# SwiGLU with stationary tokens: another order of products and output blocks, VectorE and ScalarE in written order, and a quarter of the turning transfers issued from POOL

## The chip, the core and the metric

One core of one Trainium2 chip runs the kernel. The metric is the device time in microseconds; three runs of the kernel before took 1253.64, 1248.87 and 1252.88 us, median 1252.88. TensorE (PE in the profile) multiplies, VectorE (DVE), ScalarE (ACT) and GpSimd (POOL) do the elementwise work, and SyncE (SP) issues most transfers (DMAs).

## The reference, cut to what matters

A trunk of two layers over 512 tokens of width 1024 in float32: a recurrent layer (RG-LRU), then a dilated attention layer; each ends in a SwiGLU, and the change is in that SwiGLU alone, which runs twice.

```python
D_MODEL = 1024; SEQ = 512; FFN_HIDDEN = 2816
def swiglu(h, w_in, w_out):
    g, u = jnp.split(h @ w_in, 2, axis=-1)
    return (jax.nn.silu(g) * u) @ w_out
...
h = h + swiglu(rms_norm(h, a_ffn_norm[i]), a_ffn_w_in[i], a_ffn_w_out[i])
...
h = h + swiglu(rms_norm(h, b_ffn_norm[j]), b_ffn_w_in[j], b_ffn_w_out[j])
```

## The kernel before

Every float32 operand is held as two parts, hi (rounded to the type that PE multiplies fast) and lo (the rest), and a product of two operands is three matmuls (`mm3`, L183): hi by hi, and the two mixed ones. Making the parts is called a split: ScalarE casts hi (named wh, xh, gh or T), VectorE subtracts for lo (wl, xl, gl).

`swiglu` (L581) computes 2816 hidden columns. The first 256 are done plainly (four blocks of 24 matmuls, `plain_block`); `plain_pair` applies the gate to them. The norm's factors per token come from `norm_factors` behind the first block and are spread by `norm_rows` behind the third: VectorE makes dgh and dgl (L330, L331), and PE multiplies them with ones (L335, L336) in its written order. The other 2560 columns are done in five groups of 512, counted by q from 0 to 4 and called quarters here. Each replaces the eight products of a 2 x 2 block scheme (halves of the tokens, halves of the input width, gate and up weights) by seven, with sums of weights and of inputs in their place: S1, GA, S2, GB, S3, S4 and UB. In these the tokens are stationary on PE and 512 weight columns stream, so a result has tokens in its 128 partitions. Seven products of 24 matmuls each make a quarter.

The sums of inputs are T1 to T4 (`make_t1` and so on, with d0, d1, x22 and t between); B11, B21 and B22 are parts of the input itself. The weights are fetched into GA, GB, S1, S3 and UB (`fetch`, L637); S1 and S3 take a second transfer from POOL that adds (L646), and further sums (S1 += GA for S2, GB += S1 for S4) are made on VectorE (L656), in quarter 0 by `split_weights` just ahead of the splits of S2 and S4. A product adds onto PSUM banks that an earlier one left: S2, S3 and UB onto GA's, S4 onto S1's. What stood there is copied off before (`S.copy`, L749), and behind S3 an addition reads S1's banks (L751). `gate` (L703) applies silu behind GB and S4, and `results` (L710) multiplies by the up part and turns 32 x 32 blocks on VectorE (L716).

To be the input of the product with `w_out`, the quarter's result must have its hidden columns in the partitions. `land` (L718) finishes the turn by 16 transfers of 64 KB from SBUF to SBUF (L726) into gl (in the last quarter into T2), and then splits the chunk into gh and gl (T1 and T2), four times ScalarE and four times VectorE (L729, L730). An output block O (`out_block`, L761) multiplies a piece of `w_out` by the chunk of the quarter before, and VectorE subtracts the result from the residual h (L772, in quarter 0 L774). The last chunk is multiplied by eight blocks at the very end ("last").

What sets the order: the strings in ORDERS (L40 to L42) give the order of products and O in each quarter; PE follows the written order in the whole loop (`manual_schedule`, L780). VectorE and ScalarE are put in order by a scheduler, which lets instructions marked `high_priority` (the splits of weights, the norm) go ahead. SP's and POOL's queues run in order too. `Stream` loads weight pieces four ahead and splits them two ahead; three pieces of wh and wl are in flight, so the split of a piece waits until PE has done the piece three before.

Of the kernel before, what the change touches and what calls it, by code (L numbers as in the profile page):

```python
# [15 lines left out]
F32 = mybir.dt.float32  # L16
# [3 lines left out]
AF = mybir.ActivationFunctionType  # L20
ALU = mybir.AluOpType
# [3 lines left out]
T = 512  # L25
# [147 lines left out]
def trunk(tc, A, out):  # L173
# [29 lines left out]
    class Ffn:  # L203


        def __init__(self, wi, wo, gain):
            self.gain = gain
            self.wi, self.wo = A[wi], A[wo]
            self.split = None
            self.steps = []  # L210
            for j in range(2):
                self.steps += [("plain", j, b, add_pieces([self.wi[b]])) for b in (j, HB + j)]
            for q, names in enumerate(ORDERS):
                waiting = list(range(0, 8, 2 if q else 4))
                for name in names.split():
                    if name == "O":
                        m = waiting.pop(0)
                        if q:
                            w = self.wo[m:m + 2, :, 512 * q - 256:512 * q + 256]
                        else:  # L220
                            w = self.wo[m:m + 4, :, :256]
                        self.steps.append(("out", q, m, add_pieces([w.rearrange("b q c -> q b c")])))
                    else:
# [17 lines left out]
    with tc.tile_pool(name="keep", bufs=1) as kp, tc.tile_pool(name="wts", bufs=3) as wp, \  # L241
# [339 lines left out]
        def swiglu(fp, p, after):  # L581
# [9 lines left out]
            for i, x in enumerate(sums):  # L591
                homes[f"T{i + 1}"] = [x[:, 2 * w:2 * w + 2].rearrange("q a (b t) -> q (a b) t", b=2) for w in range(2)]
            chunks = {}
            d0, d1, x22, t = (x[:, 2 * i:2 * i + 2].rearrange("q a (b t) -> q (a b) t", b=2).bitcast(F32)
                              for x in chunk() for i in range(2))
            late = slice(256, 512)

            def differences(k, dst):
# [9 lines left out]
                for i in range(4):  # L608
                    V.scalar_tensor_tensor(dst[:, i], src(i), gain(p.gain, i), x[:, i], ALU.mult, op)

            def negated(n, src):
                hi, lo = homes[n]
                S.activation(hi, src, AF.Copy, scale=-1.0)
                V.scalar_tensor_tensor(lo, src, -1.0, hi.bitcast(F32), ALU.mult, ALU.subtract)
# [33 lines left out]
            def split_weights(q, name, kk, hi, lo):  # L648
                n = name[:2]
                home = {"S2": "S1", "S4": "GB"}.get(n, n)  # L650

                def half(n):
                    return raws[q, n][:, :, 256 * kk:256 * kk + 256]

                def add(n, other):
                    V.tensor_tensor(half(n), half(n), half(other), ALU.add)  # L656

                with tc.high_priority():
                    if q == 0 and n in ("S2", "S4"):
                        add(*{"S2": ("S1", "GA"), "S4": ("GB", "S1")}[n])  # L660
                    r = half(home).rearrange("q b (k c) -> q k b c", k=2)
                    hi, lo = (x.rearrange("q (k b c) -> q k b c", k=2, b=4) for x in (hi, lo))
                    S.copy(hi, r)  # L663
                    V.tensor_tensor(lo, r, hi.bitcast(F32), ALU.subtract)  # L664
                    if q and n in ("GA", "GB"):
                        add(*{"GA": ("S1", "GA"), "GB": ("GB", "S1")}[n])
# [5 lines left out]
            p.split = split_weights  # L672
            rows, plain, acc = [], {}, {}

            def pair_tile(name="e"):
                return temps.tile([128, 2, T], F32, name=name)

            def plain_block(j, b, i):
                ps = bank("mm" if plain else "X")
                wh, wl = ws.get(i)  # L680
                for k in range(KB):
                    c = slice(128 * k, 128 * k + 128)
                    mm3(ps, (wh[:, c], wl[:, c]), (xh[k], xl[k]), k == 0, k == KB - 1)
                plain[b] = ps
                with tc.high_priority():
                    if b == 0:
                        p.r = norm_factors(fp)
                    elif b == 1:
                        rows.append(norm_rows(temps, p.r, keep=fp))

            def plain_pair(j):
                if j == 0:
# [16 lines left out]

            def results(q, half, up, part):  # L710
                if q not in turned:
                    turned[q] = fp.tile([128, 16, 4, 32], F32, name="wt", bufs=1)
                for i in range(2):
                    j = 2 * half + i
                    V.scalar_tensor_tensor(part[:, i], up[i], p.r[:, j:j + 1], part[:, i], ALU.mult, ALU.mult)  # L715
                    p.mark = V.transpose(turned[q][:, :, j], part[:, i].rearrange("q (b i) -> q b i", i=32))  # L716

            def land(q):  # L718
# [4 lines left out]
                src = turned.pop(q).rearrange("q (m b) t i -> q m b (t i)", b=4)  # L723
                for a in range(4):
                    for b in range(4):
                        nc.sync.dma_start(lo[32 * b:32 * b + 32, :, 128 * a:128 * a + 128].bitcast(F32),  # L726
                                          src[32 * a:32 * a + 32, :, b])
                for m in range(4):
                    S.copy(hi[:, m], lo[:, m].bitcast(F32))  # L729
                    V.tensor_tensor(lo[:, m], lo[:, m].bitcast(F32), hi[:, m].bitcast(F32), ALU.subtract)  # L730
# [44 lines left out]

            for n in ("GA", "GB", "S1", "S3", "UB"):
                fetch(0, n)
            early = {0: make_t1, 1: lambda: (make_t2(), make_t3()), 2: make_t4, 3: lambda: plain_pair(0),
                     4: lambda: (halve(d0, *homes["T4"]), plain_pair(1))}
            with tc.manual_schedule(engines={mybir.EngineType.PE}):  # L780
                for s, (kind, *what) in enumerate(p.steps):
                    {"plain": plain_block, "product": product, "out": out_block}[kind](*what)
                    early.get(s, lambda: None)()
# [565 lines left out]
```

## Time and profile before

| | |
|---|---|
| runs | 1253.64, 1248.87, 1252.88 us |
| the profiled execution | 1252.88 us, its span 1251.0 us, 1.9 us around it |
| PE | 5403 matmuls in the profile, busy 94% |
| VectorE, ScalarE, POOL | busy 68%, 50%, 13% |
| granted clock of PE, mean | 0.975 |
| first SwiGLU | from about 152 to 541 us of the span |
| second SwiGLU | from about 869 us to the end |

A row of a timeline gives the start in us, the duration, the engine, the line, the operation with its tiles (out<-in) and shapes, and in brackets the idle time ahead of it and what ended it. A row of the waits gives who waited for whom, the total in us, how often, and the longest. A matmul of 512 columns shows as 0.39 us but overlaps the next; what counts is the distance between starts. In the groups, "x60 | 63.2, 1054" is 60 instructions, 63.2 us busy, 1054 ns each.

### The profile page before, as it was taken

The numbers are of one execution on the slowest core, as the hardware profiler recorded it, in microseconds if no ns is written. First come the engines' busy times: TensorE is split into PE (matmuls) and PEld (weight loads), VectorE is DVE, ScalarE is ACT, GpSimd is POOL, SyncE is SP. The second block draws the span as 40 slices with busy tenths as digits, with TensorE's granted clock in tenths as the row PEclk, the third lists the DMA queues.
The fourth block names the chain that finished last, engine by engine and source line by source line (L and its number), as shares of the span: only waits on it lengthen the run. The fifth ranks groups of instructions, "written<-read, shape, count | busy, mean of one in ns | idle before, by whom it ended". The sixth has DMA issues, their size and how long they took to land.

```text
span 1251.0 us, 15052 instructions
## 1 busy us (share of the span) xinstructions
PE 1180.6 (94%) x5403; PEld 966.0 (77%) x5403; DVE 853.3 (68%) x1525; ACT 626.9 (50%) x901; POOL 166.6 (13%) x181
## 2 busy tenths in 40 slices
PE   9999998999898989799999999999998999989897
PEld 6787886777786868688888888898776877778676
DVE  8987696757575757878564676757957575757563
ACT  6795463434334343465555677646534343433431
POOL 4210011010100000010411333440110101010000
PEclk9999999999898989899999999999999999989898
DMA  7543395574655512332988667435975737464123
GB/s 245 127 121 101 101 284 155 162 181 131 167 149 153 165 51 69 101 123 89 211 183 178 136 134 169 91 77 129 260 192 147 201 110 187 130 168 134 49 65 117
DMA packets 96715, 179.61 MB, mean 144 GB/s; under 512 B 8705, under 2 KB 32129, under 8 KB 96641
## 3 DMA queue, kind: packets, MB, share of 16 engines
q1 hardware_dynamic: 77904, 132.86, 33.0%
q0 software_dynamic: 17584, 44.57, 20.6%
q10 hardware_dynamic: 1152, 1.23, 0.3%
q8 instruction: 43, 0.70, 0.2%
q14 instruction: 32, 0.25, 0.1%
HBM read 164.99 MB, written 2.10 MB: 134 GB/s over the span
## 4 chain that ended last, share of the span: by engine, by line
PE 76%; DVE 9%; ACT 6%; issue 3%; DMA 3%; SPq 2%; POOL 1%; DVEq 0%; ACTq 0%; POOLq 0%
PE ps L186 20%; PE ps L187 20%; PE ps L185 20%; PE ps L1012 5%; PE ps L1013 5%; PE ps L1014 5%; SPq L726 2%; DVE wl L664 2%; ACT wh L663 1%; ACT wh L133 1%; DVE S L656 1%; DVE xc L466 1%; PE ps L1091 1%; DVE e L715 1%; PE ps L1178 1%
## 5 line engine op out<-in xcount | busy, mean ns | idle before, releaser
L133 ACT CAST wh<-wr 128x1024 fp32r<-128x1024 f32 (+2 forms) x136 | 131.9, 970 | 182.4 <-PE ps L186 116.9
L185 PE MATMUL ps<-gh,wh 128*128 128x512 f32 x288 | 120.7, 419 | 23.7 <-ACT gh L729 18.1
L186 PE MATMUL ps<-gl,wh 128*128 128x512 f32 x288 | 121.5, 422 | 11.9 <-DVE gl L730 11.0
L663 ACT CAST wh<-S 128x1024 fp32r<-128x1024 f32 x60 | 63.2, 1054 | 126.5 <-PE ps L187 84.2
L185 PE MATMUL ps<-wh,xh 128*128 128x512 f32 x320 | 124.7, 390 | 1.9 <-DVE e L715 1.9
L187 PE MATMUL ps<-wh,xl 128*128 128x512 f32 x320 | 124.5, 389 | 0.0
L186 PE MATMUL ps<-wl,xh 128*128 128x512 f32 x320 | 124.5, 389 | 0.0
L140 DVE TENSOR_TENSOR wl<-wr,wh 128x1024 fp32r<-128x1024 f32 (+2 forms) x93 | 100.7, 1084 | 30.0 <-ACT wh L133 29.8
L646 POOL DMA_DIRECT2D S<-in_f_in x40 | 48.2, 1286 | 541.7 <-DMA S<-in_f_in 372.1
L187 PE MATMUL ps<-gh,wl 128*128 128x512 f32 x288 | 119.9, 416 | 0.0
L664 DVE TENSOR_TENSOR wl<-S,wh 128x1024 fp32r<-128x1024 f32 x60 | 73.5, 1224 | 49.4 <-ACT wh L663 49.4
L185 PE MATMUL ps<-wh,T 128*128 128x512 f32 x240 | 95.8, 399 | 6.5 <-ACT e L749 6.5
L185 PE MATMUL ps<-xh,wh 128*128 128x512 f32 x256 | 101.0, 396 | 0.5 <-ACT xh L294 0.5
L187 PE MATMUL ps<-xh,wl 128*128 128x512 f32 x256 | 100.0, 391 | 0.8 <-DMA wl<-in_w_in 0.8
L186 PE MATMUL ps<-xl,wh 128*128 128x512 f32 x256 | 100.1, 391 | 0.1
L772 DVE TENSOR_TENSOR h<-h,ps 128x512 f32<-128x512 f32 x64 | 43.7, 682 | 80.2 <-PE ps L187 80.1
L186 PE MATMUL ps<-wl,T 128*128 128x512 f32 x240 | 93.6, 390 | 0.0
L187 PE MATMUL ps<-wh,T 128*128 128x512 f32 x240 | 93.4, 389 | 0.0
L1012 PE MATMUL ps<-wh,xh 128*128 128x512 f32 x224 | 91.5, 408 | 0.0
L185 PEld LDWEIGHTS ps<-gh,wh 128*128 128x128 f32 x288 | 58.6, 204 | 41.5 <-ACT gh L729 21.5
L1014 PE MATMUL ps<-wh,xl 128*128 128x512 f32 x224 | 87.7, 392 | 0.0
L1013 PE MATMUL ps<-wl,xh 128*128 128x512 f32 x224 | 87.3, 390 | 0.0
(280 smaller groups left out, 2676.7 us busy)
## 6 DMA issues: line engine op xcount, KB each, us to landing
S<-in_f_in SPq DMA_DIRECT2D x40, 512.0 KB, 4.5
S<-in_f_in POOLq DMA_DIRECT2D x40, 512.0 KB, 7.9
wr<-in_f_out SPq DMA_DIRECT2D x36, 512.0 KB, 4.3
wr<-in_w_q SPq DMA_DIRECT2D x28, 512.0 KB, 6.8
wl<-in_w_q POOLq DMA_DIRECT2D x28, 512.0 KB, 7.6
GA<-in_f_in SPq DMA_DIRECT2D x20, 512.0 KB, 3.9
GB<-in_f_in SPq DMA_DIRECT2D x20, 512.0 KB, 6.0
UB<-in_f_in SPq DMA_DIRECT2D x20, 512.0 KB, 4.5
```

What stands on the lines that cost most here:

```text
L133: nc.scalar.copy(hi[:, c], r[:, c])
L140: a = eng.tensor_tensor(lo[:, c], r[:, c], hi[:, c].bitcast(F32), ALU.subtract)
L185: PE.matmul(ps, wh, xh, start=first, stop=False, skip_group_check=on)
L186: PE.matmul(ps, wh, xl, start=False, stop=False, skip_group_check=on)
L187: PE.matmul(ps, wl, xh, start=False, stop=last, skip_group_check=on)
L646: nc.gpsimd.dma_start(c, p.part(1, q, n == "S1", i), accum_op=ALU.add)
L663: S.copy(hi, r)
L664: V.tensor_tensor(lo, r, hi.bitcast(F32), ALU.subtract)
L772: V.tensor_tensor(by_time(x), by_time(x), in_turn(ps), ALU.subtract)
L1012: PE.matmul(ps[t], xh[k][:, r], wh[:, c], start=k == 0, stop=False)
L1013: PE.matmul(ps[t], xh[k][:, r], wl[:, c], start=False, stop=False)
L1014: PE.matmul(ps[t], xl[k][:, r], wh[:, c], start=False, stop=k == 7)
```

## The change

Three things change, all in `swiglu`. The order strings: GB now stands right behind GA in the middle quarters, two O follow S2, and a new step "L" is the place where the chunk is split (`parts_of`, taken out of `land`); the last quarter ends in three O with an L ahead of the third. The loop runs under a written order for VectorE and ScalarE as well as for PE, without the marks of priority; and T2 and T3 are made together, T4 later, with d0, d1, x22 and t in other tiles. And of the 16 turning transfers, the four with a == 0 are issued from POOL.

```diff
-MIDDLE = "S1.T1 GA.B11 S2.T2 O GB.B21 O S3.T3 O S4.B22 O UB.T4"
-ORDERS = ["GA.B11 GB.B21 O S1.T1 S2.T2 S3.T3 O S4.B22 UB.T4", MIDDLE, MIDDLE, MIDDLE,
-          "S1.T1 GA.B11 S2.T2 O GB.B21 S3.T3 O S4.B22 UB.T4 O O"]
+MIDDLE = "S1.T1 GA.B11 GB.B21 L S2.T2 O O S3.T3 O S4.B22 O UB.T4"
+ORDERS = ["GA.B11 GB.B21 O S1.T1 S2.T2 O S3.T3 S4.B22 UB.T4", MIDDLE, MIDDLE, MIDDLE,
+          "S1.T1 GA.B11 GB.B21 L S2.T2 O S3.T3 S4.B22 UB.T4 O O L O"]
...
-            d0, d1, x22, t = (x[:, 2 * i:2 * i + 2].rearrange("q a (b t) -> q (a b) t", b=2).bitcast(F32)
-                              for x in chunk() for i in range(2))
+            d = turn_tile().rearrange("q a b i -> q (a b i)").rearrange("q (w k t) -> q w k t", w=2, k=4)
+            d0, d1 = (d[:, i] for i in range(2))
+            x22, t = (quarters(pair_tile(n)) for n in ("x22", "t"))
...
-            def make_t2():
+            def make_t23():
                 gained(x22, lambda i: h[4 + i][:, late], 1)
                 combine(t, lambda i: d0[:, i], x22, ALU.add)
-                negated("T2", t)
-
-            def make_t3():
+                S.activation(homes["T2"][0], t, AF.Copy, scale=-1.0)
                 combine(x22, lambda i: h[i][:, late], x22, ALU.subtract)
-                negated("T3", x22)
+                S.activation(homes["T3"][0], x22, AF.Copy, scale=-1.0)
+
+            def low_t23():
+                for n, src in (("T2", t), ("T3", x22)):
+                    hi, lo = homes[n]
+                    V.scalar_tensor_tensor(lo, src, -1.0, hi.bitcast(F32), ALU.mult, ALU.subtract)
...
-                with tc.high_priority():
-                    if q == 0 and n in ("S2", "S4"):
-                        add(*{"S2": ("S1", "GA"), "S4": ("GB", "S1")}[n])
...
+                if q == 0 and n in ("S2", "S4"):
+                    add(*{"S2": ("S1", "GA"), "S4": ("GB", "S1")}[n])
...
-                        nc.sync.dma_start(lo[32 * b:32 * b + 32, :, 128 * a:128 * a + 128].bitcast(F32),
-                                          src[32 * a:32 * a + 32, :, b])
+                        (nc.gpsimd if a == 0 else nc.sync).dma_start(
+                            lo[32 * b:32 * b + 32, :, 128 * a:128 * a + 128].bitcast(F32), src[32 * a:32 * a + 32, :, b])
+
+            def parts_of():
+                hi, lo = chunks[max(chunks)]
                 for m in range(4):
                     S.copy(hi[:, m], lo[:, m].bitcast(F32))
                     V.tensor_tensor(lo[:, m], lo[:, m].bitcast(F32), hi[:, m].bitcast(F32), ALU.subtract)
...
-            early = {0: make_t1, 1: lambda: (make_t2(), make_t3()), 2: make_t4, 3: lambda: plain_pair(0),
-                     4: lambda: (halve(d0, *homes["T4"]), plain_pair(1))}
+            early = {0: make_t1, 1: make_t23, 2: low_t23, 3: lambda: plain_pair(0), 4: lambda: plain_pair(1),
+                     6: lambda: (make_t4(), halve(d0, *homes["T4"]))}
+            ordered = {mybir.EngineType.PE, mybir.EngineType.DVE, mybir.EngineType.Activation}
+            with tc.manual_schedule(engines=ordered):
```

The three places below name lines of their own kernel: L664, L330, L331, L601, L774 and L656 of before are L674, L332, L333, L614, L785 and L667 after the change, L729 is L740, L749 is L760 and L706 is L712.

VectorE at the start of the first SwiGLU, before: the small dependent steps of the norm (nry), then dgh and dgl, with sums for T2 and T3 (gl, here used as room for t and x22) between them and the split of GA's first piece (wl28) among them.

```order
L290 SCALAR_TENSOR_TENSOR nry_1443<-nra_1444,nry_1443 128x4
L609 SCALAR_TENSOR_TENSOR gl_1377<-h2_66,par_74,gl_1377 128x256
L330 TENSOR_SCALAR dgh_1539<-ident_75,nry_1443 128x128 x2
L331 SCALAR_TENSOR_TENSOR dgl_1540<-ident_75,nry_1443,dgh_1539 128x128 x2
L330 TENSOR_SCALAR dgh_1539<-ident_75,nry_1443 128x128
L664 TENSOR_TENSOR wl28_1512<-GA_1378,wh28_1511 128x1024
L331 SCALAR_TENSOR_TENSOR dgl_1540<-ident_75,nry_1443,dgh_1539 128x128
L330 TENSOR_SCALAR dgh_1539<-ident_75,nry_1443 128x128
L614 SCALAR_TENSOR_TENSOR T2_1374<-gl_1377,T2_1374 128x1024
L331 SCALAR_TENSOR_TENSOR dgl_1540<-ident_75,nry_1443,dgh_1539 128x128
```

The same place after the change, from T1's low parts on: the sums t and x22 for T2 and T3, then wl28, and only then the first dgh and dgl.

```order
L297 SCALAR_TENSOR_TENSOR T1_1373<-wt_1376,par_74,T1_1373 128x256 x4
L140 TENSOR_TENSOR wl27_1468<-wr27_1403,wh27_1467 128x1024
L622 SCALAR_TENSOR_TENSOR t_1378<-wt_1376,par_74,x22_1377 128x256 x4
L622 SCALAR_TENSOR_TENSOR x22_1377<-h0_64,par_74,x22_1377 128x256
L622 SCALAR_TENSOR_TENSOR x22_1377<-h1_65,par_74,x22_1377 128x256
L622 SCALAR_TENSOR_TENSOR x22_1377<-h2_66,par_74,x22_1377 128x256
L622 SCALAR_TENSOR_TENSOR x22_1377<-h3_67,par_74,x22_1377 128x256
L674 TENSOR_TENSOR wl28_1511<-GA_1379,wh28_1510 128x1024
L332 TENSOR_SCALAR dgh_1538<-ident_75,nry_1444 128x128
L333 SCALAR_TENSOR_TENSOR dgl_1539<-ident_75,nry_1444,dgh_1538 128x128
```

dgh and dgl, which PE's next matmuls read, moved behind the eight sums and behind wl28.

ScalarE in quarter 2 of the first SwiGLU, before: the copies behind GA (e_2512), S2 (e_2550), the cast of the chunk (gh, L729), and the splits of O (wr68, wr71) and GB.

```order
L663 CAST wh66_2480<-S1_2115 128x1024
L663 CAST wh67_2496<-S1_2115 128x1024
L749 COPY e_2512<-ps_2476 128x512
L133 CAST wh68_2515<-wr68_2478 128x1024
L749 COPY e_2512<-ps_2477 128x512
L663 CAST wh69_2533<-GB_2268 128x1024
L749 COPY e_2550<-ps_2476 128x512
L663 CAST wh70_2553<-GB_2268 128x1024
L749 COPY e_2550<-ps_2477 128x512
L729 CAST gh_2411<-gl_2412 128x512 x4
L133 CAST wh71_2593<-wr71_2531 128x1024
L663 CAST wh72_2611<-S3_2192 128x1024
```

The same quarter after the change, from the copies behind GA (e_2510) on; e_2510 at L712 is GB's gate, wr70 and wr71 are the two O.

```order
L760 COPY e_2510<-ps_2469 128x512
L760 COPY e_2510<-ps_2470 128x512
L673 CAST wh68_2517<-S1_2050 128x1024
L673 CAST wh69_2535<-S1_2050 128x1024
L712 ACTIVATE e_2510<-e_2510,nry_1444 128x512 x2
L740 CAST gh_2412<-gl_2413 128x512 x4
L133 CAST wh70_2563<-wr70_2515 128x1024
L133 CAST wh71_2579<-wr71_2533 128x1024
L760 COPY e_2595<-ps_2469 128x512
L760 COPY e_2595<-ps_2470 128x512
L673 CAST wh72_2600<-S3_2193 128x1024
L673 CAST wh73_2632<-S3_2193 128x1024
```

The cast of the chunk now stands behind GB's gate, and the casts of both O behind it.

VectorE in quarter 0 around the first O, before: wl34 is S1's second piece, wl35 S2's first; L656 are the additions for S2 and S4, and L774 drains O's four blocks.

```order
L705 TENSOR_TENSOR e_1637<-ps_1650,e_1637 128x512
L656 TENSOR_TENSOR S1_1384<-S1_1384,GA_1378 128x4x256
L664 TENSOR_TENSOR wl34_1689<-S1_1384,wh34_1688 128x1024
L656 TENSOR_TENSOR GB_1381<-GB_1381,S1_1384 128x4x256
L656 TENSOR_TENSOR S1_1384<-S1_1384,GA_1378 128x4x256
L705 TENSOR_TENSOR e_1637<-ps_1651,e_1637 128x512
L656 TENSOR_TENSOR GB_1381<-GB_1381,S1_1384 128x4x256
L774 TENSOR_TENSOR h0_64<-h0_64,ps_1692 128x512
L774 TENSOR_TENSOR h1_65<-h1_65,ps_1700 128x512
L774 TENSOR_TENSOR h2_66<-h2_66,ps_1708 128x512
L774 TENSOR_TENSOR h3_67<-h3_67,ps_1716 128x512
L664 TENSOR_TENSOR wl35_1727<-S1_1384,wh35_1726 128x1024
```

The same place after the change.

```order
L785 TENSOR_TENSOR h0_64<-h0_64,ps_1679 128x512
L785 TENSOR_TENSOR h1_65<-h1_65,ps_1687 128x512
L785 TENSOR_TENSOR h2_66<-h2_66,ps_1695 128x512
L785 TENSOR_TENSOR h3_67<-h3_67,ps_1703 128x512
L614 TENSOR_TENSOR wt_1376<-h4_68 128x256
L614 TENSOR_TENSOR wt_1376<-h5_69 128x256
L614 TENSOR_TENSOR wt_1376<-h6_70 128x256
L614 TENSOR_TENSOR wt_1376<-h7_71 128x256
L622 SCALAR_TENSOR_TENSOR wt_1376<-wt_1376,par_74 128x256 x4
L302 TENSOR_TENSOR xl_73<-wt_1376,xh_72 128x4x256
L667 TENSOR_TENSOR S1_1385<-S1_1385,GA_1379 128x4x256
L674 TENSOR_TENSOR wl35_1730<-S1_1385,wh35_1729 128x1024
```

Both halves of the additions stood ahead of the drains; now the drains come first, then d1 and T4 with its split (L614, L622, L302), and S1 += GA and S2's split come last.

More of the change, by code (lines that the diff above doesn't have):

```diff
@@ L222, in __init__ @@
                         self.steps.append(("out", q, m, add_pieces([w.rearrange("b q c -> q b c")])))
+                    elif name == "L":
+                        self.steps.append(("parts",))
                     else:
@@ L609, in combine @@
                     V.scalar_tensor_tensor(dst[:, i], src(i), gain(p.gain, i), x[:, i], ALU.mult, op)
[L611 to L614, printed above, removed]
             def make_t1():
@@ L656, in add @@
                     V.tensor_tensor(half(n), half(n), half(other), ALU.add)
-                with tc.high_priority():
-                    if q == 0 and n in ("S2", "S4"):
-                        add(*{"S2": ("S1", "GA"), "S4": ("GB", "S1")}[n])
[L661 to L666, printed above, removed]
+                if q == 0 and n in ("S2", "S4"):
+                    add(*{"S2": ("S1", "GA"), "S4": ("GB", "S1")}[n])
+                r = half(home).rearrange("q b (k c) -> q k b c", k=2)
+                hi, lo = (x.rearrange("q (k b c) -> q k b c", k=2, b=4) for x in (hi, lo))
+                S.copy(hi, r)
+                V.tensor_tensor(lo, r, hi.bitcast(F32), ALU.subtract)
+                if q and n in ("GA", "GB"):
+                    add(*{"GA": ("S1", "GA"), "GB": ("GB", "S1")}[n])
                 if kk:
@@ L673, in swiglu @@
             rows, plain, acc = [], {}, {}
-            def pair_tile(name="e"):
-                return temps.tile([128, 2, T], F32, name=name)
             def plain_block(j, b, i):
@@ L684, in plain_block @@
                 plain[b] = ps
[L685 to L689, printed above, removed]
+                if b == 0:
+                    p.r = norm_factors(fp)
+                elif b == 1:
+                    rows.append(norm_rows(temps, p.r, keep=fp))
             def plain_pair(j):
@@ L711, in results @@
                 if q not in turned:
-                    turned[q] = fp.tile([128, 16, 4, 32], F32, name="wt", bufs=1)
+                    turned[q] = turn_tile()
                 for i in range(2):
@@ L715, in results @@
                     V.scalar_tensor_tensor(part[:, i], up[i], p.r[:, j:j + 1], part[:, i], ALU.mult, ALU.mult)
+                for i in range(2):
+                    j = 2 * half + i
                     p.mark = V.transpose(turned[q][:, :, j], part[:, i].rearrange("q (b i) -> q b i", i=32))
```

12 lines of the change are left out of this document (9 added, 3 removed).

## Prediction

> **What bounds the kernel now.** I read the page first, then the waits of PE, then PE's timeline round each wait, then the queues of ScalarE, VectorE and SP there.
>
> ```profile
> PE 1180.6 (94%) x5403; PEld 966.0 (77%) x5403; DVE 853.3 (68%) x1525; ACT 626.9 (50%) x901; POOL 166.6 (13%) x181
> ...
> PE ps L185 <- ACT gh L729: 18.1, 8, 2.8
> PE ps L185 <- ACT T L729: 13.7, 2, 7.4
> PE ps L186 <- DVE gl L730: 11.0, 7, 1.6
> PE ps L185 <- ACT e L749: 6.5, 10, 0.6
> PE ps L185 <- DVE e L705: 5.5, 2, 2.8
> PE ps L185 <- DVE e L715: 1.9, 2, 1.0
> ```
>
> PE is the bound, and the change cannot shorten its work: the same products stand in it. It can only move waits. These six rows (total, times, longest) are 56.7 us, all of them in the two SwiGLUs. They cost more than themselves:
>
> ```profile
> 379.98 0.39 PE L187 MATMUL ps<-wh,T 128*128 128x512 f32 x1
> ...
> 384.07 0.39 PE L187 MATMUL ps<-wh,T 128*128 128x512 f32 x1
> 386.60 0.50 PE L185 MATMUL ps<-gh,wh 128*128 128x512 f32 x1 [2.14 <-ACT gh L729]
> 388.71 0.80 PE L186 MATMUL ps<-gl,wh 128*128 128x512 f32 x1 [1.61 <-DVE gl L730]
> ...
> 393.57 0.63 PE L185 MATMUL ps<-gh,wh 128*128 128x512 f32 x1
> 394.00 0.63 PE L186 MATMUL ps<-gl,wh 128*128 128x512 f32 x1
> ...
> 395.90 0.40 PE L187 MATMUL ps<-gh,wl 128*128 128x512 f32 x1
> ```
>
> This is the first output block O of one quarter. It waits for the split of the chunk that was turned at the end of the quarter before (L729, L730). After the two waits the matmuls start 0.43 us apart (393.57, 394.00) for some 5 us, and last 0.63 instead of 0.40 (395.90): PE ran at half rate. At full rate, from 379.98 to 384.07, 18 starts took 4.09 us, 0.227 each. So I count a quarter by its length:
>
> ```profile
> 244.32 0.50 PE L185 MATMUL ps<-wh,T 128*128 128x512 f32 x1 [0.65 <-ACT e L749]
> ...
> 447.57 0.50 PE L185 MATMUL ps<-wh,T 128*128 128x512 f32 x1 [0.65 <-ACT e L749]
> ...
> 959.30 0.50 PE L185 MATMUL ps<-wh,T 128*128 128x512 f32 x1 [0.65 <-ACT e L749]
> ...
> 1161.09 0.50 PE L185 MATMUL ps<-wh,T 128*128 128x512 f32 x1 [0.65 <-ACT e L749]
> ...
> 320.00:388.00 68.00, 63.67 (x264) 51.30 (x264) 43.16 (x49) 26.65 (x33) 4.83 (x4) 0.95 0.56 155
> ```
>
> The four rows are S2's first matmul in quarters 1 and 4 of both SwiGLUs, three quarters apart: 67.75 and 67.26 us a quarter. A quarter has seven products and four O of 24 matmuls, 264, which at 0.227 us are 59.9. So it loses 7.85 and 7.36 us, where idle time is only 0.65 + 3.75 = 4.4. The other 3.2 or so is half rate.
>
> **What goes away.** (1) Quarters 1 to 4, twice: 4 x (7.85 + 7.36) = 60.8. GB now stands between GA and S2, so S2 finds the copy of L749 done. O comes one product later, 21.8 us after UB's end instead of 16.3 (a product is 24 x 0.227 = 5.44). (2) The end: last waits 13.7 us in two waits for T's split; a third O hides them. With half rate behind each (0 to 3.2, as above; I take 2.2) 18.1. (3) In quarter 0 the wait of S3 for S2's copy: an O now stands there. 2 x 0.65, with the slow restart 2.4. (4) The waits for L705 and L715 round quarter 0: 7.4, with some half rate 10. Sum **91 us**.
>
> Is the chunk there in time?
>
> ```profile
> 239.41 10.40 SPq L726 DMA_DIRECT2D gl<-wt  x16
> ...
> DMA to landing us min/median/max: 2.0/2.0/3.7
> ...
> L1057 POOL DMA_DIRECT2D vl<-pl x8: 986/1002/1024, 606.6 to 617.1; - x8
> ...
> DMA to landing us min/median/max: 2.9/5.7/7.2
> ...
> L716 DVE STREAM_TRANSPOSE wt<-e 128x512 f32<-128x512 f32 x40 | 27.3, 697 | 0.0
> L715 DVE SCALAR_TENSOR_TENSOR e<-ps,nry,e 128x512 f32<-128x512 f32 x20 | 14.5, 723 | 0.0
> ```
>
> In program order two L715 and two L716 follow UB at once: 2.8 us. SP then issues 12 transfers instead of 16, 12 x 0.65 = 7.8, landing 2.0: 12.6 after UB. POOL's four have the nearest row in 64 KB copies of the attention: 4 x 1.0 to issue, 2.9 to 7.2 to land, so 9.7 to 14.0. L is due when GB and its gate are done, at 16.3 + 1.6 = 17.9. The slack is 3.9 us, so the quarter given to POOL is priced at nothing. All 16 on SP would be in time at 15.2. On SP the turning transfers now stand ahead of GA's fetch; GA is needed a quarter later, so that costs nothing. Behind POOL's four stands S1's sum for the next quarter, which is due 40 us later.
>
> Behind L, the splits of the first O stand on both engines in order:
>
> ```profile
> L663 ACT CAST wh<-S 128x1024 fp32r<-128x1024 f32 x60 | 63.2, 1054 | 126.5 <-PE ps L187 84.2
> L749 ACT COPY e<-ps 128x512 f32<-128x512 f32 x60 | 35.0, 583 | 28.1 <-PE ps L187 28.1
> L706 ACT ACTIVATE e<-e,nry 128x512 f32<-128x512 f32 x40 | 26.9, 714 | 7.4 <-DVE e L705 7.4
> ...
> 882.20 1.21 DVE L664 TENSOR_TENSOR wl<-GA,wh 128x1024 fp32r<-128x1024 f32 x1
> 883.34 1.21 DVE L614 SCALAR_TENSOR_TENSOR T<-gl,T 128x1024 fp32r<-128x1024 f32 x1
> ```
>
> From GB's end: gate until 1.6, four gh 3.75, wh of O 4.75, its wl (1.14 from start to start, as the last two rows) 6.0. O is due at 5.4 and needs wl at its third matmul, 5.9. So each of eight quarters keeps about 0.3: 2.4. In quarter 4, S3 and S4 now touch. S4 adds onto the bank that the add behind S3 reads: copy 0.58, add 0.7, less the overlap 0.9, with restart 1.4, twice 2.8. The end keeps 0.6. **New there: 5.8.**
>
> **What quarter 0 pays.** The order that the scheduler made there put urgent work first; the written order does not.
>
> ```profile
> 155.88 1.43 DVE L601 TENSOR_TENSOR gh<-h 128x256 f32<-128x256 f32 x4
> ...
> 158.68 0.16 DVE L318 TENSOR_SCALAR nrv<-ps 128x4 f32<-128x4 f32 x1
> ...
> 168.66 1.06 ACT L613 ACTIVATE T<-gl 128x1024 fp32r<-128x1024 f32 x1 [3.54 <-DVE gl L609]
> ...
> 171.04 1.71 ACT L605 ACTIVATE gh<-gh,par 128x256 f32<-128x256 f32 x4
> ...
> 169.53 0.40 PE L335 MATMUL ps<-dgh,ones_r 128*128 128x512 f32 x1
> ...
> 880.37 0.47 DVE L330 TENSOR_SCALAR dgh<-ident,nry 128x128 fp32r<-128x128 f32 x2
> ```
>
> The steps below are these durations, one behind the other on the engine that runs them: a cast wh 1.05, a split wl 1.14, an add or product of 512 columns 0.6 to 0.7, of 256 columns 0.36 (1.43 for four) or 0.40 on VectorE and 0.41 to 0.5 on ScalarE, and 0.05 to 0.1 for a hand-over, an estimate that I take from no single row.
>
> (a) dgh and dgl, which PE reads at 169.53 (L335) without a wait, now stand behind T1, T2's and T3's sums and the split wl28. From nrv at 158.68: eight dependent small steps at 0.2 to 160.4, four differences 161.8, T1's low parts, held by ScalarE, 163.1, wl27 164.7, eight sums at 0.40 167.95, ScalarE's T3 (1.06) and wh28 170.1, wl28 171.25, dgh and dgl (880.37 to 882.20: 1.83) 173.1. PE goes on at 173.6 instead of 169.99: 3.6.
>
> (b) The first O of quarter 0. Its fourth block takes the bank of its first, which L774 must have drained. In the written order L774 stands behind wl34, wl34 behind wh34, that behind GB's gate. From GA's end: the plain pair's product w*g 2.05, gh 3.15, gl 4.35, wl32 5.5, wl33 6.6, gate adds 7.9, silu 8.65, wh34 9.65, wl34 10.8, first L774 11.4. Block four was due at 9.5: 2.0.
>
> (c) Behind L774 stands all of T4 and its split: the last L774 13.7, differences 15.1, combined 16.7, xh 17.8, xl 19.0, S1 += GA 20.1, wh35 21.2, wl35 22.4. S1 ends at 18.3, so S2 waits 2.95, then 0.75 more, and 0.65 for wl36 behind a second addition: 4.4, with hand-overs 4.6.
>
> (d) S4 needs GB += S1 twice and the copies behind S3, which wait for wh41. From S2's end: last L774 6.2, addition 7.4, wh40 8.5, wl40 9.7, addition 10.8, wh41 11.9, copy 12.5, wl41 and the first add 13.7. S4 was due at 10.9: 2.9.
>
> (e) S1 of quarter 1 is fetched after that second addition, and summed by POOL's transfer:
>
> ```profile
> S<-in_f_in SPq DMA_DIRECT2D x40, 512.0 KB, 4.5
> S<-in_f_in POOLq DMA_DIRECT2D x40, 512.0 KB, 7.9
> ```
>
> 10.85 + 0.45 + 4.5, then 1.0 to issue as in L1057 and 7.9: its second half is there at 24.7, and wh44, wl44 bring it to 26.8; S1 is due at 24.6 (10.9 + 2.9 + two products): 2.2.
>
> Idle 3.6 + 2.0 + 4.6 + 2.9 + 2.2 = 15.3 a pass. Nothing hides it, since PE runs in order. Half rate comes on top: bounds 0 and 3.2 after (a), (c) and (d), 0 and 2 after the shorter two. I take 2.4, 1.5, 1.2, 0.3 and 0.6, 6.0 in all, nearest to what the quarter's row shows for its longest pair and less for single waits, as (c)'s slow stretch also covers part of its own waits. Twice 21.3 is **42.6**.
>
> The Trainium skill, "TensorE: Matmul & The Clock Gate", section "What's actually happening", says that the clock halves after a whole idle window of about 3.4 us. The trace disagrees: 2.14 and 1.61 with a matmul between brought the 0.43 us spacing. By the page only (a) would be followed by half rate, and the sum would be 7 us lower.
>
> **The sum.** The profiled run took 1252.88 us, which is the median as well: 1252.9 - 91 + 42.6 + 5.8 = 1210.
>
> **Rivals.**
>
> ```profile
> 908.24 0.50 PE L185 MATMUL ps<-gh,wh 128*128 128x512 f32 x1 [2.71 <-DVE e L705]
> 908.57 0.40 PE L186 MATMUL ps<-gl,wh 128*128 128x512 f32 x1
> ```
>
> *Half rate needs longer waits*: (b) to (e) then cost only themselves, 2 x 3.6 less, 1203. For it speaks this wait of 2.71 us, behind which the matmuls are 0.40 long at once; against it the quarter's rows. Chance 0.15. *Quarter 0 stays covered*: if ScalarE and VectorE hand over faster or data arrive earlier, so that (c) to (e) mostly vanish, 2 x 11 us go: 1188. Against it: each chain is of full-length rows. 0.12. *Order costs in the middle too*: some further split in each of eight quarters is 1 to 2 us late with half rate behind it: 8 x 2.5, 1230. VectorE has 43 us of work in a quarter of 60, so it has room. 0.13. *The added order changes nothing on balance*: the quarters keep half their loss, 1247. 0.04. *Slower*: L holds ScalarE and VectorE, and so every split behind it, until the last transfer has landed. If POOL's land over 17.9 after UB by w, a quarter loses w + 2.5 of half rate; eight of them eat the gain of 43 at w = 2.9, which is a landing at 20.8, a last transfer of 14 us after its issue. The worst row is 7.2. At 18 us w is 6.9 and the time 1285. 0.05. The forecast itself, 1200 to 1222, has 0.51.
>
> **How the numbers follow.** The range takes in the bounds on half rate (1198 to 1224), most of the covered case and of the middle case: 1188 to 1231. A measurement of this kernel tells 0.5%, about 6 us, from no change. Faster by more than that 0.91, within 0.04, slower 0.05.
>
> **What would show it.** Right: waits for L729 and L730 gone, quarters 1 to 4 of about 60.3 us from S2 to S2, PE waiting at L335 for 3 us, S2 of quarter 0 waiting for S1's split, S4 for the add behind S3. Wrong: gh of L waiting for transfers, or a quarter above 62; a quarter 0 without waits.

## The result and the profile after

The changed kernel took 1215.5 us (median of 4 runs, 1214.6 to 1218.2), the kernel before 1251.1 beside it: ratio 0.972, 95% interval 0.969 to 0.975. The prediction said 1210, between 1188 and 1231. The profiled execution took 1215.45, its span 1213.6, the mean granted clock 0.987.

The head of the page of the changed kernel:

```profile
PE 1171.2 (97%) x5403; PEld 961.5 (79%) x5403; DVE 854.5 (70%) x1525; ACT 622.2 (51%) x901; POOL 188.3 (16%) x221
```

The waits of PE there, longest first:

```profile
PE ps L337 <- DVE dgh L332: 7.9, 2, 4.0
PE ps L185 <- DVE e L762: 7.5, 4, 3.0
PE ps L185 <- ACT wh L673: 7.0, 3, 2.9
PE ps L185 <- DVE h L785: 3.3, 2, 1.7
PE ps L186 <- DVE wl L674: 2.0, 3, 0.8
...
PE ps L186 <- DVE T L741: 1.1, 1, 1.1
...
PE ps L185 <- DVE h L783: 0.9, 1, 0.9
```

All six rows of before are gone (gh, gl and T of L729 and L730, e of L749, L705 and L715; of the waits for T's split one of 1.1 us is left, now for its low part, L741). In their place stand the five waits that the prediction listed as (a) to (e): L337 is (a), L785 (b), wh and wl of L673 and L674 (c) and (e), e of L762 (d).

PE's timeline of the changed kernel: S2's first matmul in quarters 1 and 4 of both SwiGLUs, and in the first SwiGLU the start of each of (a), (c), (d) and (e):

```profile
174.11 0.59 PE L337 MATMUL ps<-dgh,ones_r 128*128 128x512 f32 x1 [3.92 <-DVE dgh L332]
...
174.93 0.63 PE L185 MATMUL ps<-xh,wh 128*128 128x512 f32 x1
175.35 0.63 PE L186 MATMUL ps<-xl,wh 128*128 128x512 f32 x1
...
208.61 0.79 PE L185 MATMUL ps<-wh,T 128*128 128x512 f32 x1 [2.88 <-ACT wh L673]
...
231.99 0.51 PE L185 MATMUL ps<-wh,xh 128*128 128x512 f32 x1 [3.03 <-DVE e L762]
...
245.99 0.49 PE L185 MATMUL ps<-wh,T 128*128 128x512 f32 x1 [1.22 <-ACT wh L673]
...
263.48 0.39 PE L185 MATMUL ps<-wh,T 128*128 128x512 f32 x1
...
445.85 0.39 PE L185 MATMUL ps<-wh,T 128*128 128x512 f32 x1
...
960.08 0.39 PE L185 MATMUL ps<-wh,T 128*128 128x512 f32 x1
...
1142.45 0.39 PE L185 MATMUL ps<-wh,T 128*128 128x512 f32 x1
```

From 263.48 to 445.85 and from 960.08 to 1142.45 three quarters take 182.37 us, 60.8 each, where they took 67.75 and 67.26. The rows at 174.93 and 175.35, behind (a), show half rate: starts 0.42 us apart.

Below, the **excess** of a place is the sum by which matmuls start more than 0.227 us after the one before; it holds idle time and half rate together (an even spacing of 0.233, as O's below, is not counted). Added up over the timeline of both SwiGLUs it was 93.2 us before and is 49.8 now. By it the terms of the prediction come out so (us, first / second SwiGLU):

| | predicted, a pass | measured |
|---|---|---|
| (a) rows dgh, dgl | 6.0 | 5.8 / 7.0 |
| (b) drain of the first O | 2.3 | 2.0 / 2.0 |
| (c) S2's split behind T4 | 6.1 | 6.7 / 5.6 |
| (d) S4 behind the add | 4.1 | 4.9 / 6.1 |
| (e) fetch of the next S1 | 2.8 | 2.5 / 0.4 |
| quarter 0, both passes | 42.6 | 42.8 |
| middle and end, both passes | 5.8 | 7.0 |

So 93.2 - 42.8 - 7.0 = 43.4 us should have gone; 37.4 went in the profiled executions. O's matmuls hold nearly all of the missing 6. One O in the middle of quarter 1, changed kernel:

```profile
285.85 0.40 PE L185 MATMUL ps<-gh,wh 128*128 128x512 f32 x1
...
291.21 0.39 PE L187 MATMUL ps<-gh,wl 128*128 128x512 f32 x1
291.44 0.39 PE L185 MATMUL ps<-wh,xh 128*128 128x512 f32 x1
```

24 matmuls without a wait take 5.59 us, 0.233 each. Before, O's ran at 0.227 like all others, and the products still do. Over 2 x 432 matmuls of O that is 5.4 us. The prediction had no such term. In the built program the chunk's tiles moved: gh from address 0x20880 to 0x32200 in the first SwiGLU and from 0x1f080 to 0x30a00 in the second, since the chunk is now set aside last. The new places are multiples of 256, those of the other operands that PE streams are not (wh at 0x13080, xh at 0x8080).

Two things were to be tested: what slows O, and whether the account behind the terms holds (the order of products gains, the written order costs). The table only shows that the sum fits.

### The profile page after: what moved, and what is told of

The parts are those of the page before. It is cut to its first block, busy times and chain, and to the rows that moved or that the text cites. A ratio compares the mean times of both kernels' runs of the same rounds, so it can differ in the third digit from the quotient of the medians.

```text
span 1213.6 us, 15155 instructions
## 1 busy us (share of the span) xinstructions
PE 1171.2 (97%) x5403; PEld 961.5 (79%) x5403; DVE 854.5 (70%) x1525; ACT 622.2 (51%) x901; POOL 188.3 (16%) x221
## 4 chain that ended last, share of the span: by engine, by line
PE 82%; DVE 9%; ACT 4%; DMA 3%; issue 2%; POOL 0%; DVEq 0%; ACTq 0%; POOLq 0%
PE ps L187 22%; PE ps L186 22%; PE ps L185 22%; PE ps L1025 5%; PE ps L1026 5%; PE ps L1027 5%; DMA S<-in_f_in 2%; DVE wl L674 1%; ACT wh L673 1%; PE ps L1104 1%; PE ps L1191 1%; DVE wl L140 1%; DVE xc L468 1%; ACT wh L133 1%; ACT pr L1177 0%
## 5 line engine op out<-in xcount | busy, mean ns | idle before, releaser
L185 PE MATMUL ps<-gh,wh 128*128 128x512 f32 x288 | 113.9, 396 | 3.3 <-DVE h L785 3.3
L187 PE MATMUL ps<-gh,wl 128*128 128x512 f32 x288 | 114.6, 398 | 0.3
L186 PE MATMUL ps<-gl,wh 128*128 128x512 f32 x288 | 113.7, 395 | 0.0
L674 DVE TENSOR_TENSOR wl<-S,wh 128x1024 fp32r<-128x1024 f32 x60 | 73.3, 1225 | 47.2 <-ACT wh L673 47.2
L185 PE MATMUL ps<-xh,wh 128*128 128x512 f32 x256 | 103.5, 406 | 1.0 <-ACT xh L296 1.0
L673 ACT CAST wh<-S 128x1024 fp32r<-128x1024 f32 x60 | 62.8, 1050 | 79.3 <-PE ps L186 21.9
L673 ACT CAST wh<-GB 128x1024 fp32r<-128x1024 f32 x40 | 42.1, 1054 | 76.1 <-PE ps L187 50.9
```

The source lines that it names most:

```text
L185: PE.matmul(ps, wh, xh, start=first, stop=False, skip_group_check=on)
L186: PE.matmul(ps, wh, xl, start=False, stop=False, skip_group_check=on)
L187: PE.matmul(ps, wl, xh, start=False, stop=last, skip_group_check=on)
```

## The experiments

The kernel before took 1253.0 to 1253.7 us in the three sets of runs. "A to B" is the 95% interval of the ratio to it.

### Where gh and gl lie

```diff
-            chunks = {}
+            chunks = {0: chunk()}
...
-                    chunks[0] = chunk()
```

> The changed kernel with the chunk tiles gh and gl set aside first, so that they lie where they lay before the change (at 0x20880 in the first SwiGLU, not 0x32200); nothing else moves but the tiles behind them. Theory A (where gh and gl lie sets the rate of O's matmuls): O's matmuls start 0.2267 us apart again instead of 0.2330, 864 of them or more, about 5.4 us less: 1210. Theory B (O is slower because of what runs beside it now that two O touch, or because of the order): spacing stays at 0.2330 and the time at 1215.5.

And, without that edit:

```diff
+                    pad = fp.tile([128, 32], F32, name="pad", bufs=1)
+                    G.memset(pad, 0.0)
                     chunks[0] = chunk()
```

> The changed kernel with 128 bytes left free ahead of gh (one small memset on POOL more), so that gh lies at 0x32280, 128 bytes off a multiple of 256 like all operands before, but still in the upper part of the memory. If the place modulo 256 counts: O at 0.2267 us a matmul, 1210. If the upper part counts: 0.2330 and 1215.5. If neither: 1215.5 as well, and the run with the low place says which.

The same O with the low tiles, PE's timeline:

```profile
284.38 0.39 PE L185 MATMUL ps<-gh,wh 128*128 128x512 f32 x1
...
289.82 0.39 PE L185 MATMUL ps<-wh,xh 128*128 128x512 f32 x1
```

and with the 128 bytes ahead of gh:

```profile
286.86 0.39 PE L185 MATMUL ps<-gh,wh 128*128 128x512 f32 x1
...
292.30 0.39 PE L185 MATMUL ps<-wh,xh 128*128 128x512 f32 x1
```

Both take 5.44 us, 0.227 a matmul. The padded tiles are still in the upper part of the memory, so the place modulo 256 decides, not the region. Low tiles at a multiple of 256 were not tried.

Yet the times hardly moved: 1214.2 (0.966 to 0.972) and 1216.6 (0.967 to 0.973). The first SwiGLU got 2.6 us shorter with the low tiles (from the mean square's first matmul to the next one's, 364.3 to 361.7), the second 3.3 longer. There quarter 0's excess rose from 21.0 to 26.9: (d) fell from 6.1 to 3.3, but (e) went from 0.4 to 9.1. SP's queue with the low tiles:

```profile
921.91 0.91 SPq L655 DMA_DIRECT2D S<-in_f_in  x2
...
930.42 1.45 SPq L655 DMA_DIRECT2D UB<-in_f_in  x2
```

ScalarE there, at S1's split:

```profile
940.81 1.99 ACT L673 CAST wh<-S 128x1024 fp32r<-128x1024 f32 x2 [8.45 <-DMA S<-in_f_in]
```

and SP's queue of the changed kernel, second SwiGLU:

```profile
926.51 0.93 SPq L655 DMA_DIRECT2D S<-in_f_in  x2
...
937.46 1.15 SPq L655 DMA_DIRECT2D UB<-in_f_in  x2
```

With the low tiles UB's fetch was issued 8.5 us behind S1's instead of 11.0, just when POOL issued the second half of S1's sum; that second half took 10.2 us to land instead of 6.5. In the changed kernel half rate behind (d) had held PE, and with it the split that releases UB, some 3 us longer. So a slower PE had hidden a late fetch. That the two transfers slow each other is what the traces suggest: over both passes of six kernels (the changed one, the low tiles, the 128 bytes, all 16 on SP, and the two single moves in quarter 0 below) the second half took 9.9 to 10.7 us in the three passes in which UB's fetch was issued no later than it, and 6.5 to 8.8 in the nine in which UB's came 0.8 to 3.3 us later. It was not measured alone.

### The quarter given to POOL

```diff
-                        (nc.gpsimd if a == 0 else nc.sync).dma_start(
+                        nc.sync.dma_start(
```

> The changed kernel with all 16 turning transfers issued from SP. My sum prices POOL's quarter at nothing: within 1 us of 1215.5, the last landing some 2.5 us later, still ahead of L. Rival (POOL's quarter is what makes L possible): gh of L waits for transfers, and each of eight quarters loses 1 to 3 us: 1224 to 1240.

1218.2 us (0.969 to 0.973): 2.7 us more, where within 1 was expected, though the interval overlaps that of the changed kernel. No wait for gh came, so the middle quarters don't need POOL. The last chunk of the second SwiGLU does; ScalarE and PE there:

```profile
1188.98 2.18 ACT L740 CAST T<-T 128x512 fp32r<-128x512 f32 x4 [10.40 <-DMA T<-wt]
...
1189.65 0.50 PE L185 MATMUL ps<-T,wh 128*128 128x512 f32 x1 [0.29 <-ACT T L740]
```

SP issues 16 transfers from 1175.60 on, and T's split starts 13.4 us behind the first of them; in the changed kernel, with 12 on SP, it starts 10.2 us behind (1174.36 to 1184.52), and PE does not wait there. By excess the ends of both SwiGLUs cost 2.6 us more with all 16 on SP.

### L at once

```diff
-MIDDLE = "S1.T1 GA.B11 GB.B21 L S2.T2 O O S3.T3 O S4.B22 O UB.T4"
+MIDDLE = "L S1.T1 GA.B11 GB.B21 S2.T2 O O S3.T3 O S4.B22 O UB.T4"
...
-          "S1.T1 GA.B11 GB.B21 L S2.T2 O S3.T3 S4.B22 UB.T4 O O L O"]
+          "L S1.T1 GA.B11 GB.B21 S2.T2 O S3.T3 S4.B22 UB.T4 O O L O"]
```

> The changed kernel with step L written as the first step of quarters 1 to 4 instead of behind GB. If the written order holds ScalarE and VectorE at L until the last transfer lands (the mechanism of my slower case): landing at about 13 us behind UB's end, four gh and gl 3, then GA's split 2: GA, due 5.4 us behind UB, starts at about 18; eight times 12 us and half rate behind: 1310 to 1340. If these engines pass over an instruction that waits: no change, 1215.

1316.8 us in a single run. ScalarE:

```profile
258.64 2.18 ACT L740 CAST gh<-gl 128x512 fp32r<-128x512 f32 x4 [13.64 <-DMA gl<-wt]
260.72 1.99 ACT L673 CAST wh<-GA 128x1024 fp32r<-128x1024 f32 x2
```

The waits of PE:

```profile
PE ps L185 <- ACT wh L673: 86.0, 11, 10.9
```

ScalarE stands 13.6 us idle at L, and GA's split behind it starts as soon as L is done. Of the 86 us, 6 are quarter 0's; the eight quarters wait 10.0 each and lose 12.7, (1316.8 - 1215.5) / 8, half rate included. The mechanism of the slower rival is real; L's place behind GB keeps it away.

### The order of products alone

The kernel before with the new strings:

```diff
-MIDDLE = "S1.T1 GA.B11 S2.T2 O GB.B21 O S3.T3 O S4.B22 O UB.T4"
-ORDERS = ["GA.B11 GB.B21 O S1.T1 S2.T2 S3.T3 O S4.B22 UB.T4", MIDDLE, MIDDLE, MIDDLE,
-          "S1.T1 GA.B11 S2.T2 O GB.B21 S3.T3 O S4.B22 UB.T4 O O"]
+MIDDLE = "S1.T1 GA.B11 GB.B21 S2.T2 O O S3.T3 O S4.B22 O UB.T4"
+ORDERS = ["GA.B11 GB.B21 O S1.T1 S2.T2 O S3.T3 S4.B22 UB.T4", MIDDLE, MIDDLE, MIDDLE,
+          "S1.T1 GA.B11 GB.B21 S2.T2 O S3.T3 S4.B22 UB.T4 O O O"]
```

> The kernel before with the new order of products and units alone (the ORDERS strings without L): the scheduler still orders ScalarE and VectorE, the chunk is still split where it lands, all turning transfers on SP, tiles where they were. Theory A (the order of products alone takes the waits of quarters 1 to 4 and of the end; the written order only costs, in quarter 0): 79 + 2 less, some 3 to 6 for the new touches: 1173 to 1180, O at 0.2267 us. Rival B (without the written order the scheduler puts splits or the chunk's parts in bad places, so the written order is needed for the gain): 1215 or more.

1203.8 us (0.959 to 0.964): neither theory's time, and 12 us below the changed kernel. Its waits of PE:

```profile
PE ps L185 <- DVE e L751: 8.1, 8, 1.3
PE ps L185 <- DVE e L705: 5.5, 2, 2.8
PE ps L186 <- DVE gl L730: 5.0, 6, 0.8
PE ps L185 <- ACT T L729: 4.0, 2, 2.7
PE ps L185 <- ACT gh L729: 3.4, 2, 1.7
PE ps L185 <- DVE e L715: 1.9, 2, 0.9
```

The order takes 49 us, more than the whole change (36), but it leaves waits for the chunk, for the gate (L705) and for the add behind S3 (L751).

### Only PE in written order

```diff
-            ordered = {mybir.EngineType.PE, mybir.EngineType.DVE, mybir.EngineType.Activation}
+            ordered = {mybir.EngineType.PE}
```

> The changed kernel with only TensorE in written order: the scheduler orders ScalarE and VectorE again, but without the urgency marks that the change took out. Theory A (the written order costs 43 us in quarter 0, nothing else): the waits (a) to (e) shrink, 1175 to 1195. Rival B (the marks count, not the written order): quarter 0 keeps its waits and new ones come, 1210 or more.

**1172.2 us** (0.934 to 0.938), 43.3 less than the changed kernel and below even theory A's range. Its waits of PE in the SwiGLUs are two rows:

```profile
PE ps L185 <- DVE e L762: 2.9, 4, 0.7
PE ps L186 <- DVE T L741: 2.2, 2, 2.0
```

The granted clock is 1.000: none of the waits that are left, at most 2.0 us long, brought half rate. VectorE of the changed kernel at (a):

```profile
159.19 0.16 DVE L320 TENSOR_SCALAR nrv<-ps 128x4 f32<-128x4 f32 x1 [2.84 <-PE ps L318]
...
165.22 1.67 DVE L622 SCALAR_TENSOR_TENSOR t<-wt,par,x 128x256 f32<-128x256 f32 x4
...
170.54 1.23 DVE L674 TENSOR_TENSOR wl<-GA,wh 128x1024 fp32r<-128x1024 f32 x1 [2.06 <-ACT wh L673]
171.68 0.28 DVE L332 TENSOR_SCALAR dgh<-ident,nry 128x128 fp32r<-128x128 f32 x1
```

and with only PE in written order:

```profile
157.91 0.16 DVE L320 TENSOR_SCALAR nrv<-ps 128x4 f32<-128x4 f32 x1
157.99 0.47 DVE L297 SCALAR_TENSOR_TENSOR T<-wt,par,T 128x256 fp32r<-128x256 f32 x1
...
163.26 0.48 DVE L332 TENSOR_SCALAR dgh<-ident,nry 128x128 fp32r<-128x128 f32 x2
...
164.38 1.23 DVE L674 TENSOR_TENSOR wl<-GA,wh 128x1024 fp32r<-128x1024 f32 x1
```

dgh starts 5.4 us behind nrv instead of 12.5. The written order waited 2.84 us for nrv and 2.06 us for wh with other work behind; the scheduler put sums there, and between the small steps of the norm.

### The marks, and L

The same kernel with `tc.high_priority()` again around the splits of the summed weights and around the mean squares and rows:

```diff
+                with tc.high_priority():
                     if q == 0 and n in ("S2", "S4"):
...
+                with tc.high_priority():
                     if b == 0:
```

> Only TensorE in written order, with the urgency marks that the change took out put back on the splits of the summed weights and on the mean squares and rows. The kernel before with the new order of products took 1204, with these marks, without L; TensorE alone in written order took 1172, without the marks, with L. Theory A (the marks pull splits ahead of the gates and the sums, and these come late): 1190 or more, with waits for L711, L723 or the silu's result. Theory B (L makes the difference): 1172.

1189.9 us (0.946 to 0.951). Waits of PE:

```profile
PE ps L185 <- DVE e L764: 8.1, 8, 1.3
PE ps L185 <- DVE e L713: 5.3, 2, 2.7
```

The add behind S3 (L764) and the gate (L713) come late again, 8.1 and 5.3 us, as with the order alone (8.1 and 5.5). The marks cost 17.6 us: they were not what protected quarter 0.

The same without marks, and the chunk split in `land` instead of at L:

```diff
+                parts_of()
...
-MIDDLE = "S1.T1 GA.B11 GB.B21 L S2.T2 O O S3.T3 O S4.B22 O UB.T4"
+MIDDLE = "S1.T1 GA.B11 GB.B21 S2.T2 O O S3.T3 O S4.B22 O UB.T4"
...
-          "S1.T1 GA.B11 GB.B21 L S2.T2 O S3.T3 S4.B22 UB.T4 O O L O"]
+          "S1.T1 GA.B11 GB.B21 S2.T2 O S3.T3 S4.B22 UB.T4 O O O"]
```

> Only TensorE in written order, and the chunk split where it lands, with no step L. Theory A (the marks make the difference): 1172 to 1176. Theory B (without L the scheduler puts the chunk's four splits late or in front of the gate, as with the new order alone, where O waited 0.84 to 2.5 us for gh and gl, and T 2.7): 1185 or more.

1171.3 us (0.931 to 0.936): L is worth nothing where the scheduler orders the two engines.

### One place of quarter 0 at a time

```diff
-            early = {0: make_t1, 1: make_t23, 2: low_t23, 3: lambda: plain_pair(0), 4: lambda: plain_pair(1),
-                     6: lambda: (make_t4(), halve(d0, *homes["T4"]))}
+            early = {0: make_t1, 2: lambda: (make_t23(), low_t23()), 3: lambda: plain_pair(0),
+                     4: lambda: plain_pair(1), 6: lambda: (make_t4(), halve(d0, *homes["T4"]))}
```

> The changed kernel with T2's and T3's sums written behind the rows dgh and dgl instead of ahead of them (with their low parts, one step later). Step (a) of the prediction: the wait at the rows' matmul, 3.9 us and its half rate, goes: 6 us less in each SwiGLU, 1203, if nothing behind it comes late instead. Rival (the sums are in the way of the splits wherever they stand): the wait moves to the next split or to the first O, and the time stays within 3 us of 1215.

1208.0 us (0.962 to 0.967). No wait at the rows is left: (a)'s excess went from 12.7 us over both passes to 2.8. But (e)'s rose from 2.9 to 8.7: of the 9.9 us, the late fetch took 5.8 back, so both theories have a part. (b) rose by 2.0 and (c) and (d) fell by 4.8 together, mostly with where half rate fell.

```diff
-                     6: lambda: (make_t4(), halve(d0, *homes["T4"]))}
+                     8: lambda: (make_t4(), halve(d0, *homes["T4"]))}
```

> The changed kernel with T4 and its split written behind S2 instead of behind the first O. Step (c): S2 no longer waits for its split (2.9 and 0.5 to 0.8 us, with half rate 5.6 to 6.7): 10 to 12 us less in all, 1204. Rivals: T4 now stands ahead of S3's and S4's splits, and (d) grows by what (c) loses (1213 to 1217); or S4 comes sooner and the fetch of the next S1 is late instead (e), as with the low tiles in the second SwiGLU, where it took 9 us: 1208 to 1215.

1216.5 us (0.968 to 0.974). (c) went, as expected, but its place was taken. PE's timeline, second O of quarter 0 and S1 of quarter 1, both in the second SwiGLU:

```profile
912.21 0.50 PE L185 MATMUL ps<-gh,wh 128*128 128x512 f32 x1 [2.68 <-DVE h L785]
...
939.53 0.80 PE L185 MATMUL ps<-wh,T 128*128 128x512 f32 x1 [6.01 <-ACT wh L673]
```

The drain of the second O now stands behind T4, which I had not foreseen, and S1's fetch is late, which the second rival said; (d) did not grow.

All together, quarter 0 as "GA GB S1 S2 O S3 O S4 UB", the rows first, T4 behind S3 and low tiles:

```diff
-ORDERS = ["GA.B11 GB.B21 O S1.T1 S2.T2 O S3.T3 S4.B22 UB.T4", MIDDLE, MIDDLE, MIDDLE,
+ORDERS = ["GA.B11 GB.B21 S1.T1 S2.T2 O S3.T3 O S4.B22 UB.T4", MIDDLE, MIDDLE, MIDDLE,
...
+            early = {0: make_t1, 2: lambda: (make_t23(), low_t23()), 3: lambda: plain_pair(0),
+                     4: lambda: plain_pair(1), 9: lambda: (make_t4(), halve(d0, *homes["T4"]))}
```

> All three engines in written order, but quarter 0 written otherwise: GA GB S1 S2 O S3 O S4 UB, the rows ahead of T2's and T3's sums, T4 behind S3; gh and gl set aside first. Theory A (the written order costs what its places cost, not because it is written): (a) goes, (c) goes, an O stands between S2 and S3 and between S3 and S4, so (d) goes, and S1's fetch has one O more (e): 34 of 43 us and O's 5.4 go, 1176 to 1185. Rival (VectorE has no room in quarter 0 for these units in any fixed order): waits of the same size elsewhere, 1200 or more.

1189.9 us (0.946 to 0.951), 24 less than with the low tiles alone, but short of theory A's range. Waits of PE:

```profile
PE ps L185 <- DVE h L784: 13.6, 2, 6.8
```

(a), (c), (d) and (e) are gone but for splits under 1 us late; one large wait of 6.8 us a pass is left, again an O's drain behind T4. It costs 19.2 us over both passes with half rate. So a written order costs what its places cost, but I found no place for T4 that costs nothing, and whether there is one stays open.

### The best version

Only PE in written order, and gh and gl set aside first:

```diff
-            ordered = {mybir.EngineType.PE, mybir.EngineType.DVE, mybir.EngineType.Activation}
+            ordered = {mybir.EngineType.PE}
...
-            chunks = {}
+            chunks = {0: chunk()}
```

> Only TensorE in written order, and gh and gl set aside first (0x20880 instead of 0x32200). If a place at a multiple of 256 bytes costs O 0.0063 us a matmul by itself, the 864 matmuls or more of O give back 5.4 us, and here no late fetch can take them, since quarter 0 has no wait for one: 1172 becomes 1167. Rival (what O gains is again taken elsewhere): 1172.

**1164.8 us** (0.926 to 0.930), against 0.934 to 0.938 without the low tiles. From mean square to mean square the first SwiGLU takes 339.0 us instead of 342.4; of the 3.4, 0.5 are another wait for T. The rest, 2.9, is about O's 2.7, here without a fetch to take it.

## Why the prediction was right, and where its account was not

**What goes away**, 91 us, was 93.2 by excess. Each listed wait went, and the quarters came to 60.8 us against 60.3 or so; the difference is O's slower rate, 4 x 24 x 0.0063 = 0.6. But I put the whole of it down to the order of products. The order alone brings 49 of it with the scheduler as it was; the waits for L705 and for the chunk, which I thought the order would hide, stay until the marks are gone (17.6 us) and the rest of the change is in (the kernel with marks, L, POOL's quarter and moved sums is 14 us below the order alone, though its O is slower). Which of the moved sums and tiles does that was not tried.

**What quarter 0 pays**, 42.6 us, was 42.8 by excess, and 43.3 when the written order was taken off VectorE and ScalarE. (a) to (c) came within 1.0 us each, (d) was 0.8 and 2.0 over, and (e) 0.3 and 2.4 under. That the sum came out within 0.2 is luck: (d)'s error and (e)'s cancel. And (e) is not a size but a race: 0.4 to 9.2 us over these runs, by when UB's fetch falls. The hand-over of 0.05 to 0.1 us, which the prediction took from no row, is at its low end or below in the trace of before: from the end of one instruction to the start of the one that waited for it, a median of 0.03 us between ScalarE and VectorE and 0.05 to 0.06 from either to PE. The reason given, that the scheduler put urgent work first, was half wrong. At (a), without the marks, its order fills waits with sums that are ready, and the marks only made the time longer.

**New there**, 5.8 us, was 7.0: eight quarters 0.31 each against 0.3, S3 to S4 1.0 against 1.4, the end 2.5 in the first SwiGLU and nothing in the second against 0.6 in all. In the first, VectorE makes tables for the next layer (L876 to L904) between the start of T's casts (488.59) and that of its low parts (492.08).

**POOL's quarter at nothing** held for the eight middle quarters. At the two ends, for which the prediction has no such sum, it is worth some 2.6 us by the profiles.

**The sum** missed by 5.5 us, and the step that failed is its first sentence on PE: that the change "cannot shorten" PE's work and "can only move waits". It lengthened that work: it moved gh and gl, and O's 864 matmuls took 0.233 us instead of 0.227, 5.4 us.

**The rivals.** "Half rate needs longer waits" (1203) fell: it came behind 3.92, behind 2.88 with 0.47 more, and behind 3.03 us, though not behind each such wait (2.20 with 0.77 and 3.05 us in the second SwiGLU with the low tiles were followed by none). What decides is where a wait falls. Each row below is a stretch of 3.41 us with PE's busy time and, third from the right, the granted clock; the first two are the changed kernel's at (d), the others those of the low tiles round the wait of 3.05 us.

```profile
228.93:232.34 3.41, 0.38 (x3) 0.31 (x3) 2.24 (x3) 2.96 (x4) 0.00 (x0) 1.00 1.12 201
232.34:235.75 3.41, 3.41 (x10) 2.63 (x9) 1.32 (x2) 0.00 (x0) 0.54 (x1) 0.50 1.04 387
...
920.19:923.60 3.41, 1.71 (x8) 1.09 (x6) 2.22 (x3) 1.61 (x3) 0.32 (x1) 1.00 1.08 172
923.60:927.02 3.42, 2.07 (x9) 1.72 (x10) 3.02 (x4) 1.35 (x2) 0.00 (x0) 1.00 1.06 259
```

In each trace that has half rate it starts only on one even grid of 3.413 us (in the changed kernel at 174.32, 208.45, 232.34, 870.64, 908.18 and 928.66, whole multiples apart) and lasts one to four of its steps. In the SwiGLUs of the fourteen traces, all 59 steps at full clock in which PE idled 1.96 us or more were followed by half rate; of the 2715 in which it idled less than 1.79 us, one was; between the two values both happened. The wait of 3.03 us lay in one step, that of 3.05 us is cut into 1.70 and 1.35. So a wait of 2 to 3 us brings half rate or not by where it falls on the grid, which the prediction's single prices for half rate could not tell. The Trainium skill, "TensorE: Matmul & The Clock Gate", section "What's actually happening", has the clock halve after an idle window of about 3.4 us, in windows that run freely. The traces agree on the length of the windows and that they run freely (the grid above), but the idle window need not be idle throughout: here 1.96 us of idle time in one were enough. "Covered" (1188) did not happen, "slower" needs L where the chunk is not there yet, as the run with L at once shows.

## What to carry to other kernels

Ask of a change made of several parts which part pays: here the order of products, the end of the marks and the moved sums made about 80 us together, and the written order of two helper engines gave 43 back. Before fixing an engine's order by hand, list what stands behind each instruction that waits; a drain or a short step of a chain behind a batch of sums stops the engine that bounds the kernel. When tiles move, compare the start distances of the same matmuls before and after.

## What the runs showed of the hardware

Streaming operands (gh and gl) at a multiple of 256 bytes made a 128 x 512 float32 matmul start every 0.233 us (eight traces), and at 128 bytes past one every 0.227 (six traces); the upper part of the memory by itself cost nothing. Half rate (0.43 us a matmul) came in whole steps of a grid of 3.413 us, behind each step in which PE idled 1.96 us or more, and with only PE in written order, where no wait of the SwiGLUs was longer than 2.0 us, the granted clock was 1.000.
